# Two modulation vectors moved behind the recurrent stage, row vectors through DRAM, and norm operands made by ScalarE

## The chip, the cores and the metric

The kernel runs as one program on one core of one Trainium2 chip. The metric is the device time of one execution in microseconds (us). The engines named here are TensorE (PE in the profile), VectorE (DVE), ScalarE (ACT), GpSimd (POOL) and the queue of SyncE (SP), which only issues transfers from DRAM.

## The reference, cut to what matters

Two models of two layers each run one after the other on 256 tokens of 1024 channels, in fp32.

```python
# first model, layer 0; layer 1 has shared_kv + attention in place of rglru_mixer
mod = silu(c) @ mod_w[l] + mod_b[l]                      # (1, 6*1024)
sh_m, sc_m, g_m, sh_f, sc_f, g_f = split(mod, 6)
h = rmsnorm(x, norm_mix[l]) * (1 + sc_m) + sh_m
mix = rglru_mixer(h, ...)     # h@w_in, conv of 4, gates, a recurrence over tokens, @w_out
x = x + g_m * mix
h = rmsnorm(x, norm_ffn[l]) * (1 + sc_f) + sh_f
x = x + g_f * swiglu(h, ...)  # h@w_gate, h@w_up, @w_down
# second model, each layer: eight norms that have a gain and no shift
f = swiglu_2(rmsnorm_2(h, g[0]), ...);  h = h + 0.5 * rmsnorm_2(f, g[1])
mix = hybrid_mixer(rmsnorm_2(h, g[2]), ...);  h = h + rmsnorm_2(mix, g[3])
f = swiglu_2(rmsnorm_2(h, g[4]), ...);  h = h + 0.5 * rmsnorm_2(f, g[5])
gate = sigmoid(rmsnorm_2(h, g[6]) @ w_ple_gate[i])
h = h + rmsnorm_2((p[i] @ w_ple[i]) * gate, g[7])
```

Fourteen modulation vectors come out of `silu(c)`: six for each layer of the first model and two for `shared_kv`. The kernel numbers them v0 to v13 (`MODS`, line 173). v0 and v1 are scale and shift of the first norm, v2 is the gate `g_m` of layer 0, v3 and v4 are scale and shift of its feed-forward norm, v5 its gate `g_f`; v6 and v7 belong to `shared_kv`, v8 to v13 to layer 1.

## The kernel before, in words

**Weights.** All weights are one stream of 266 chunks of 128x2048 f32 (1 MB each), loaded in order by SP into four slots (`raw<-in_ws`). Of each half chunk ScalarE makes the high part (`whi<-raw`), and VectorE the low part (`wlo<-raw,whi`); five slots of each. A product in fp32 is three matmuls: high by high, high by low, low by high. The activations that a matmul reads are split in the same way into one buffer, `xhl`.

**Stages.** They follow each other as the weight stream has them: `lx` (w_in, with the conv of 4), `lg` (gates), `ly` (the other half of w_in, with the recurrence), `lo` (w_out), `b0pl` (an embedding product that only layer 0 of the second model needs), `gu0`, `dn0` (feed-forward of layer 0), `b1pl`, `kv`, `kk`, `aq`, `ao` (attention of layer 1), `gu1`, `dn1`; and then, for each layer l of the second model, `b{l}gu0`, `b{l}dn0`, `b{l}vd`, `za`, `zb`, `kn`, `vm`, `q`, `b{l}o`, `b{l}gu1`, `b{l}dn1`, `b{l}pg`. Stages like `lo`, `dn0`, `ao` end with a norm (a "boundary"): x is updated, normed, transposed on PE through a PSUM bank, multiplied by a gain (`gained`, 8 places in the second model, each for 2 token tiles and 2 halves) or by scale and shift (`modulate`), and split into `xhl`, which the first matmul of the next stage reads.

**The norm's operands.** `spread` (line 1065) does that last step. For a gain, VectorE multiplies 128x512 from the bank into a buffer `n`, ScalarE copies it to the high part (`xhl<-n`), VectorE subtracts for the low part. For scale and shift VectorE multiplies and adds; only four of these blocks, at the very start, are made by ScalarE in 128x128 pieces with scale and bias as pointers (`by_scalar`).

**Modulation vectors.** Each has a weight of 1024x1024 (`in_wm`), loaded 1 MB at a time into `raw` slots (for v0 and v1, in part, into tiles that the recurrent stage uses later, `part`). v0 to v4 are made by PE (`mod_pe`: groups of four products `bank<-raw,cs 32x512`), the others by VectorE. Columns (scale, shift) lie one channel a partition. Rows (the gates v2, v5, v10, v13, `MOD_ROW`) are wanted on all 128 partitions: `mod_row` accumulates on VectorE, and `row_sum` adds over partitions by fp32 matmuls with ones or halves, 128x512, two a vector. `JOBS` and `JOB_AT` (lines 174 and 176) set their order and the chunk at which each may begin.

**Order.** Nothing is issued as written. A `Recorder` collects all instructions, and `order` (line 481) places them by modelled costs (`cost_of`, `TABLE_LOAD`) and due times, each engine with its own list. Where PE's modelled wait is over 1 us and a PSUM bank is free, `keep_busy` (line 607) fills it with matmuls of ones on ones (`bank<-ones`), which compute nothing that is read; in the trace they stand at line 1253, two records for each instruction. Nearly all other instructions stand at line 687, the line of the recording helper, so the rows are told apart by operands.

**Paired units.** In `lx` a PSUM bank holds two units of 256 columns, of which `steps` evicts each as soon as its own sum is finished; the other unit's matmuls go to the same bank.

Of the kernel before, what the change touches and what calls it, by code (L numbers as in the profile page):

```python
# [108 lines left out]
def plan():  # L109
# [8 lines left out]
    for l in range(2):  # L118
        ph[f"b{l}pl"] = moving(2, lambda a, u, k, l=l: rows(a["w_ple_2"][l], k, span(u)), 1, 8)
        if l == 1:  # L120
            ph["kv"] = moving(KD, lambda a, u, k: rows(a["w_kv"], k, span(4 + u)))
            ph["kk"] = dense(4, KD, lambda a, u, k: rows(a["w_kv"], k, span(u)))
            ph["aq"] = dense(KD, KD, lambda a, u, k: rows(a["attn_w_q"][0], k, span(u)))
            ph["ao"] = moving(KD, lambda a, u, k: rows(a["attn_w_o"][0], k, span(u)), 1, 8)
        ph[f"gu{l}"] = gate_up("ffn_w_gate", "ffn_w_up", l)
        ph[f"dn{l}"] = moving(KF, lambda a, u, k, l=l: rows(a["ffn_w_down"][l], k, span(u)), 1, 8)
# [45 lines left out]
JOBS = [(0, 0), (1, 0), (0, 1), (1, 1), (2, 0), (2, 1), (3, 0), (3, 1), (4, 0), (4, 1)]  # L172
JOBS += [(v, 0) for v in (6, 7, 8, 9, 5, 10, 11, 12, 13)]
JOB_AT = [0, 0, 0, 0, 5, 5, 5, 5, 5, 5, 18, 22, 26, 30, 35, 41, 46, 51, 66]
# [7 lines left out]
def mod_stream(a):  # L182
    out = []
    for v, i in MOD_PART:
# [4 lines left out]
        elif v in MOD_ROW:  # L189
            w = w.reshape(4, 2, P, D)  # L190
        else:
            w = w.T.reshape(4, 2, P, D)
# [190 lines left out]
class Recorder:  # L383
# [97 lines left out]
    def order(self):  # L481
# [49 lines left out]
        while total:  # L531
            best = None
            for e, lst in pending.items():
                tmin, cand = None, []
                for o in lst[:48]:
# [5 lines left out]
                    if o.table and not o.table & table:  # L541
                        t += TABLE_LOAD
# [17 lines left out]
            t, e, o = best  # L560
            if o.table:
                table = table & o.table or set(o.table)
            total -= 1
            pending[e].remove(o)
            o.start, o.end = t, t + o.cost
# [165 lines left out]
class Program:  # L731
# [15 lines left out]
    def memory(self, ctx):  # L747
# [12 lines left out]
        self.pls = dram.tile([4, P, D], FT, name="pls")  # L760

# [117 lines left out]
    def start_job(self):  # L879
# [4 lines left out]
        return self.mod_row(v) if v in MOD_ROW else self.mod_col(v)  # L884
# [22 lines left out]
    def mod_row(self, v):  # L907
        nc = self.nc
        acc = self.row()
        bias = None  # L910
        for part in range(4):
            raw = self.mod_raw(v, 0, part, 0.0)
            if part == 3:
                bias = [self.mod_bias(v, h) for h in range(2)]
            for s in range(2):
                k = part * 2 + s
                w, col = raw[:, s * D:(s + 1) * D], self.cs[:, k:k + 1]
                if k == 0:
                    nc.vector.tensor_scalar(acc, w, col, None, op0=OP.mult)
                else:  # L920
                    nc.vector.scalar_tensor_tensor(acc, w, col, acc, op0=OP.mult, op1=OP.add)
            if part < 3:
                yield
        for h in range(2):
            self.row_sum(v, h, acc[:, h * 512:(h + 1) * 512], self.ones if MODS[v][2] == 2 else self.halves, acc,
                         bias[h])

    def mod_bias(self, v, h):
        b = self.wide()
        i = 9 + MOD_ROW.index(v)  # L930
        self.nc.sync.dma_start(b[:1], self.ins["rows"][i:i + 1, h * 512:(h + 1) * 512])
        return b

    def row_sum(self, v, h, acc, by, out, b):

        nc = self.nc
        nc.vector.tensor_add(acc[:1], acc[:1], b[:1])
        ps = self.bank()
        nc.tensor.matmul(ps, by, acc, start=True, stop=True)
        nc.scalar.activation(out[:, h * 512:(h + 1) * 512], ps, AF.Copy)  # L940
        self.mod_rows[v] = out

# [6 lines left out]
    def mod_pe(self, v, i):  # L949
# [4 lines left out]
        bias = self.mod_bias(v, i) if v in MOD_ROW else None  # L954
# [4 lines left out]
        self.mod_sums(v, i, ps, bias)  # L959

    def mod_sums(self, v, i, ps, bias=None):
# [16 lines left out]
    def mod_done(self, v, sums, o, n):  # L978
# [5 lines left out]
        if (kind == "kv" and j == 1) or (kind == "m" and j in (1, 4)):  # L984
            g = self.vec("kn", o, n) if kind == "kv" else self.vec("nm" if j == 1 else "nf", l * 8 + o, n)
            nc.vector.scalar_tensor_tensor(m, m, 1.0, g, op0=OP.add, op1=OP.mult)

# [21 lines left out]
    def steps(self, name, x, evict, at=lambda k, u: k, each=1):  # L1009
# [3 lines left out]
        seen, ps = {}, {}  # L1013
        for j, (u, k) in enumerate(p.order):
# [10 lines left out]
            if seen[u] == p.nk:  # L1025
                evict(u, ps[u][:, :T])
                yield u
# [27 lines left out]
    def turned(self, t, src, outs, k0=0):  # L1055

        self.spread(t, self.transposed(src), outs, k0)
# [7 lines left out]
    def spread(self, t, xt, outs, k0, by_scalar=False):  # L1065
        nc = self.nc
        n = xt.shape[1] // P
        for dst, g, sh in outs:
            u = xt[:, :n * P]
            bc = lambda c: c[:, k0:k0 + n, None].to_broadcast([P, n, P])  # L1070
            if by_scalar:
                v = self.wide(n * P)
                for j in range(n):
                    a = slice(j * P, (j + 1) * P)
                    nc.scalar.activation(v[:, a], u[:, a], AF.Identity, scale=g[:, k0 + j:k0 + j + 1],
                                         bias=sh[:, k0 + j:k0 + j + 1])
# [870 lines left out]
```

## Time and profile before

| | |
|---|---|
| time, median of 3 runs | 1696.34 us (1695.57 to 1697.22) |
| profiled execution | 1695.63 us, span 1693.8 us |
| granted TensorE clock, mean | 0.999 |
| busy share PE, DVE, ACT, POOL | 98%, 70%, 52%, 4% |
| matmuls of ones on ones | 248 records (124 instructions) |
| DMA | 353.02 MB, 208 GB/s mean |
| stage `lx` | 27.7 to 70.7 us of the span |
| stage `ly` | 89.7 to 130.7 |
| stage `lo` | 130.7 to 164.5 |
| stage `b0pl` | 164.5 to 173.8 |
| stage `gu0` | 173.8 to 305.8 |
| stage `ao` | 436.5 to 464.8 |

A busy PE is any matmul, those of ones included. Times of stages were read from PE's own order of instructions. The columns of the views are told at each group of rows below.

### The profile page before, as it was taken

To read this page: it belongs to the slowest core of one execution; us is meant where nothing else is said; L and a number is where in the kernel's file an instruction comes from. 1 tells how busy PE (TensorE), PEld (TensorE's weight loads), DVE (VectorE), ACT (ScalarE), POOL (GpSimd) and SP (SyncE) were. 2 spreads that over 40 slices of the span, in tenths; PEclk is the share of its full clock that TensorE was granted. 3 is DMA by queue.
4 is the path that set the end of the run, shared out by engine and by line. 5 is a ranking of instruction groups with operands and counts; after the bars stand their busy time and mean duration, and the time that the engine had idled before them with its cause. 6 is when DMAs were issued, how large, how long until landed. Compare 5 with 4: busy or idle time off the path is not lost.

```text
span 1693.8 us, 22563 instructions
## 1 busy us (share of the span) xinstructions
PE 1663.0 (98%) x8698; PEld 1383.3 (82%) x8698; DVE 1180.3 (70%) x1912; ACT 878.3 (52%) x1319; POOL 65.0 (4%) x97
## 2 busy tenths in 40 slices
PE   7999999999999999999999999999999999999997
PEld 4887888779878887888889788887888889888886
DVE  3879999888786656666478866548665477865646
ACT  3785444455644445455367544437544356554434
POOL 0000000010000000000000100001000000000001
PEclk9999999999999999999999999999999999999999
DMA  9577799986465554555442565445555542365451
GB/s 390 201 291 264 295 358 350 356 306 228 149 232 182 195 178 168 207 191 180 168 175 88 183 227 199 174 174 188 204 180 182 191 174 88 150 239 196 174 199 62
DMA packets 51019, 353.02 MB, mean 208 GB/s; under 512 B 5957, under 2 KB 6093, under 8 KB 9696
## 3 DMA queue, kind: packets, MB, share of 16 engines
q1 hardware_dynamic: 46960, 338.73, 54.2%
q0 software_dynamic: 3520, 11.60, 2.0%
q8 instruction: 68, 1.11, 0.3%
q10 hardware_dynamic: 432, 1.26, 0.2%
q14 instruction: 39, 0.32, 0.1%
HBM read 348.41 MB, written 3.16 MB: 208 GB/s over the span
## 4 chain that ended last, share of the span: by engine, by line
PE 64%; DVE 5%; issue 1%; ACT 1%; DMA 0%; POOL 0%; POOLq 0%; DVEq 0%; ACTq 0%
PE bank L687 64%; DVE wlo L687 2%; DVE n L687 1%; DVE x L687 1%; DVE xhl L687 0%; ACT n L687 0%; DMA raw<-in_wm_dram 0%; DVE macc L687 0%; ACT whi L687 0%; DVE part L687 0%; POOL sm L687 0%; DVE sm L687 0%; POOLq L1943 0%; DVEq L1943 0%; ACT xhl L687 0%
## 5 line engine op out<-in xcount | busy, mean ns | idle before, releaser
L687 DVE TENSOR_TENSOR wlo<-raw,whi 128x1024 fp32r<-128x1024 f32 (+1 forms) x577 | 651.6, 1139 | 372.3 <-ACT whi L687 370.5
L687 ACT ACTIVATE whi<-raw 128x1024 fp32r<-128x1024 f32 (+1 forms) x577 | 565.2, 992 | 539.4 <-PE bank L687 483.3
L687 PE MATMUL bank<-whi,xhl 128*128 128x512 f32 x2208 | 703.0, 394 | 1.7 <-DVE xhl L687 0.8
L687 PEld LDWEIGHTS bank<-whi,xhl 128*128 128x128 f32 x2208 | 413.1, 188 | 91.8 <-DVE xhl L687 4.5
L687 PE MATMUL bank<-whi,part 128*128 128x512 f32 x1464 | 460.4, 392 | 0.0
L687 PE MATMUL bank<-wlo,xhl 128*128 128x512 f32 x1104 | 431.7, 391 | 2.5 <-DVE wlo L687 2.2
L687 PEld LDWEIGHTS bank<-whi,part 128*128 128x128 f32 x1464 | 274.4, 188 | 58.6 <-ACT part L687 1.4
L687 PE MATMUL bank<-wlo,part 128*128 128x512 f32 x732 | 286.2, 392 | 1.2 <-DVE wlo L687 1.0
L687 PEld LDWEIGHTS bank<-wlo,xhl 128*128 128x128 f32 x1104 | 207.5, 188 | 47.2 <-DVE wlo L687 6.0
L687 PEld LDWEIGHTS bank<-wlo,part 128*128 128x128 f32 x732 | 137.6, 188 | 30.4 <-DVE wlo L687 2.5
L687 PE MATMUL bank<-xhl,whi 128*128 128x256 f32 x768 | 144.8, 287 | 0.0
L687 PEld LDWEIGHTS bank<-xhl,whi 128*128 128x128 f32 x768 | 120.4, 191 | 10.9 <-issue 6.4
L687 PE MATMUL bank<-xhl,wlo 128*128 128x256 f32 x384 | 108.9, 286 | 2.6 <-ACT part L687 2.6
L687 ACT ACTIVATE n<-bank 128x512 f32<-128x512 f32 (+2 forms) x116 | 60.4, 531 | 85.0 <-PE bank L687 81.8
L687 POOL TENSOR_TENSOR sm<-sm,mhalf 128x1 f32<-128x1 f32 (+1 forms) x52 | 41.8, 810 | 1339.3 <-DVE sm L687 1232.1
L687 PE MATMUL bank<-ident,n 128*128 128x128 f32 x512 | 81.8, 276 | 4.2 <-DVE n L687 4.2
L687 PEld LDWEIGHTS bank<-ident,n 128*128 128x128 f32 x512 | 63.2, 143 | 23.8 <-DVE n L687 7.0
L687 PEld LDWEIGHTS bank<-xhl,wlo 128*128 128x128 f32 x384 | 73.4, 191 | 4.0 <-ACT part L687 3.4
L687 ACT ACTIVATE part<-bank 128x512 fp32r<-128x512 f32 (+3 forms) x96 | 50.0, 528 | 39.5 <-PE bank L687 37.9
L687 DVE TENSOR_TENSOR part<-bank,part 128x512 fp32r<-128x512 f32 (+3 forms) x122 | 65.5, 551 | 3.4 <-PE bank L687 2.9
L687 DVE SCALAR_TENSOR_TENSOR n<-n,bank 128x512 f32<-128x512 f32 (+1 forms) x82 | 50.0, 612 | 12.8 <-ACT n L687 12.7
L687 DVE CUSTOM_DVE_ANT_0 raw<-raw,macc 128x1024 f32<-128x1024 f32 x48 | 57.1, 1221 | 0.1
(155 smaller groups left out, 1156.2 us busy)
## 6 DMA issues: line engine op xcount, KB each, us to landing
raw<-in_ws_dram SPq DMA_DIRECT2D x266, 1024.0 KB, 4.8
raw<-in_wm_dram SPq DMA_DIRECT2D x48, 1024.0 KB, 6.9
part<-in_wm_dram SPq DMA_DIRECT2D x8, 1024.0 KB, 12.9
macc<-in_rows_dram POOLq DMA_DIRECT2D x10, 512.0 KB, 4.3
pls<-n POOLq DMA_DIRECT2D x8, 256.0 KB, 4.4
macc<-pls POOLq DMA_DIRECT2D x4, 512.0 KB, 5.8
x<-in_x_dram ACTq DMA_DIRECT2D x2, 512.0 KB
n<-scr POOLq DMA_DIRECT2D x8, 128.0 KB, 7.0
```

What stands on the lines that cost most here:

```text
L687: getattr(getattr(rec.nc, name), method)(*[real(v) for v in args], **{k: real(v) for k, v in kw.items()})
```

## The change

1. The work of v3 and v4 leaves the job list. Their weights are loaded after the recurrent tiles come free: four parts into these tiles (`through`), four into `raw` slots, and their products, sums and the norm's operands are written behind `lo`. The stage `b0pl` moves from behind `lo` to behind `ao`, in the weight stream too.
2. All four row vectors are made as columns and spread: GpSimd writes the columns to a DRAM scratch `modr` (elements of 4 bytes) and reads it back as one row for 128 partitions. `mod_row`, `row_sum` and their bias loads go.
3. `steps` with two units in a bank evicts both when both are finished.
4. `spread` for a gain: ScalarE makes the high part from the bank in four 128x128 pieces with the gain as a pointer, VectorE the low part in four pieces. For scale and shift at a `turn_x` boundary ScalarE makes four pieces with two pointers in place of VectorE's multiply and add.
5. The scheduler charges the load of an activation table to the instruction that needs it, in place of delaying that instruction as a candidate.

```diff
-JOBS = [(0, 0), (1, 0), (0, 1), (1, 1), (2, 0), (2, 1), (3, 0), (3, 1), (4, 0), (4, 1)]
+JOBS = [(0, 0), (1, 0), (0, 1), (1, 1), (3, 0), (4, 0), (3, 1), (4, 1), (2, 0), (2, 1)]
...
-                    if o.table and not o.table & table:
-                        t += TABLE_LOAD
                     cand.append((t, o))
...
+            load = TABLE_LOAD if o.table and not o.table & table else 0.0
+            o.start, o.end = t, t + load + o.cost
...
@@ mod_done
+        if v in MOD_ROW:
+            if j == 5:
+                nc.vector.tensor_scalar(m, m, 0.5, None, op0=OP.mult)
...
+            dst = bass.AP(tensor=self.modr.tensor, offset=self.modr.offset + i * D + o * P, ap=[[1, P], [P, n]])
...
+            nc.add("gpsimd", lambda: self.nc0.gpsimd.dma_start(dst, m.real()), [row], [m], 0.6, 3.0)
+            if o + n == KD:
+                self.mod_rows[v] = self.row()
+                src = bass.AP(tensor=self.modr.tensor, offset=self.modr.offset + i * D, ap=[[0, P], [1, D]])
...
@@ steps
-            if seen[u] == p.nk:
-                evict(u, ps[u][:, :T])
-                yield u
+            if seen[u] < p.nk:
+                continue
+            done.append(u)
+            if each == 1 or all(seen.get(v, 0) == p.nk for v in range(u - u % each, u - u % each + each)):
+                for v in done:
+                    evict(v, ps[v][:, :T])
+                    yield v
+                done = []
@@ spread
+            if g is not None and sh is None:
+                for a, k in cols:
+                    nc.scalar.activation(hi[:, a], u[:, a], AF.Copy, scale=g[:, k])
+                    nc.vector.scalar_tensor_tensor(lo[:, a], u[:, a], g[:, k], hi[:, a].bitcast(FT), op0=OP.mult,
+                                                   op1=OP.subtract)
+                continue
...
@@ lru
-        then = self.modulate([(h, self.mod("m", 0, 4), self.mod("m", 0, 3))], 8.0)
+        through = [b.flat()[:, :CH * P] for b in (tt, ig, q, xc)]
...
+        load(4)
...
         self.natural("lo", Tall(yh), self.add_gated(gate, then), halves=2, tail=self.TAIL)
-        self.embed(0)
+        load(8)
+        out = [(h, *(self.mods[:, v * 8:(v + 1) * 8] for v in (3, 4)))]
+        for i in range(2):
+            for v in (3, 4):
+                ps = self.bank()
+                for part in range(2):
+                    self.mod_products(ps, raw[v, i, part], part)
+                self.mod_sums(v, i, ps)
...
```

What this does to the order is shown at three places. On PE, from the end of `lo` to the first matmuls of `gu0` (those that read `xhl`), before and after. `wlo_73` in `b0pl`'s rows is the buffer that holds its token operand; `cs` is `silu(c)`.

```order
L687 MATMUL bank_132<-whi_71,part_4_165 128x512
L687 MATMUL bank_136<-macc_128,sm_94 8x384
L1253 MATMUL bank_134<-ones 128x128 x10
L687 MATMUL bank_134<-whi_67,wlo_73 128x512
L687 MATMUL bank_134<-wlo_72,wlo_73 128x512
L687 MATMUL bank_131<-whi_67,wlo_73 128x512
```

```order
L687 MATMUL bank_136<-wlo_74,wlo_73 128x512
L687 MATMUL bank_136<-whi_68,wlo_73 128x512
L687 MATMUL bank_130<-ident,n_115 128x128 x4
L687 MATMUL bank_133<-ident,n_116 128x128 x4
L1253 MATMUL bank_135<-ones 128x128 x12
L687 MATMUL bank_135<-whi_69,xhl_77 128x512
```

```order
L685 MATMUL bank_136<-whi_71,part_4_166 128x512
L685 MATMUL bank_132<-ident,n_118 128x128 x4
L685 MATMUL bank_129<-part_3_165,cs 32x512 x4
L685 MATMUL bank_129<-part_0_162,cs 32x512 x4
L685 MATMUL bank_130<-raw_66,cs 32x512 x3
L685 MATMUL bank_134<-ident,n_113 128x128 x4
L685 MATMUL bank_130<-raw_66,cs 32x512
L685 MATMUL bank_130<-raw_64,cs 32x512
L685 MATMUL bank_135<-ident,n_111 128x128 x4
L685 MATMUL bank_130<-raw_64,cs 32x512 x3
L685 MATMUL bank_133<-ident,n_114 128x128 x4
L685 MATMUL bank_131<-raw_63,cs 32x512
```

The first fence is the end of `lo` and the start of `b0pl`, the second the end of `b0pl` and the start of `gu0`, with 10 and 12 matmuls of ones; the third is the same place in the changed kernel, where products of v3 and v4 and the norm's transposes stand behind `lo`, and neither `b0pl` nor a matmul of ones.

On the queue of SP, the transfers that reach from `ly` to `gu0` (`in_wm` is a modulation weight, `in_ws` the stream; `part_0` to `part_3` are the recurrent tiles).

```order
L687 DMA raw_63<-in_ws_dram 128x2048
L687 DMA raw_65<-in_wm_dram 128x2048
L687 DMA raw_64<-in_wm_dram 128x2048
L687 DMA raw_66<-in_wm_dram 128x2048
L687 DMA raw_63<-in_ws_dram 128x2048
L687 DMA raw_65<-in_ws_dram 128x2048
```

```order
L685 DMA raw_65<-in_ws_dram 128x2048
L685 DMA part_1_163<-in_wm_dram 128x2048
L685 DMA part_2_164<-in_wm_dram 128x2048
L685 DMA part_3_165<-in_wm_dram 128x2048
L685 DMA part_0_162<-in_wm_dram 128x2048
L685 DMA raw_66<-in_wm_dram 128x2048
L685 DMA raw_64<-in_wm_dram 128x2048
L685 DMA raw_63<-in_wm_dram 128x2048
L685 DMA raw_66<-in_wm_dram 128x2048
L685 DMA raw_64<-in_ws_dram 128x2048
```

Before, modulation weights lie between chunks of the stream; in the changed kernel eight of them stand in one run, behind the last chunk of `lo` and ahead of the first of `gu0` (`raw_64<-in_ws`, last row).

On PE, from `b0pg` to `b1gu0`, a boundary with a gain, before and after (`x` is the updated residual, `xhl_77` the next stage's operand).

```order
L687 MATMUL bank_136<-whi_69,part_0_7267 128x512
L1253 MATMUL bank_131<-ones 128x128 x4
L687 MATMUL bank_131<-ident,x 128x128 x4
L687 MATMUL bank_129<-ident,x 128x128 x4
L1253 MATMUL bank_133<-ones 128x128 x8
L687 MATMUL bank_133<-whi_70,xhl_77 128x512
```

```order
L685 MATMUL bank_133<-whi_69,part_0_7308 128x512
L1232 MATMUL bank_130<-ones 128x128 x4
L685 MATMUL bank_130<-ident,x 128x128 x4
L685 MATMUL bank_129<-ident,x 128x128 x4
L685 MATMUL bank_134<-whi_70,xhl_77 128x512
L685 MATMUL bank_134<-wlo_76,xhl_77 128x512
```

The eight matmuls of ones between the transposes and the first matmul of the next stage are gone. Over the whole program the matmuls of ones fall from 124 instructions to 51, the fp32 row sums from 8 to none, and PE's transposes of `n` rise from 512 to 520; ScalarE gets 1392 instructions in place of 1216, VectorE 1987 in place of 1914, GpSimd nine more transfers.

## Rows read from the trace of the kernel before

**Rows 1.** The page: span, and PE's busy time, share and instructions.
```profile
span 1693.8 us, 22563 instructions
PE 1663.0 (98%) x8698; PEld 1383.3 (82%) x8698; DVE 1180.3 (70%) x1912; ACT 878.3 (52%) x1319; POOL 65.0 (4%) x97
```

**Rows 2.** Windows: stretch, length; busy us (instructions) per engine; granted clock; DMA share; GB/s.
```profile
7.00:15.00 8.00, 3.87 (x16) 0.40 (x16) 2.77 (x19) 2.45 (x8) 0.56 (x1) 1.00 1.02 426
...
89.70:130.70 41.00, 40.77 (x322) 32.25 (x320) 31.14 (x68) 34.22 (x70) 0.04 (x1) 1.00 0.76 277
130.70:164.50 33.80, 33.80 (x175) 28.05 (x172) 31.58 (x61) 17.47 (x29) 1.58 (x3) 1.00 0.70 264
164.50:173.80 9.30, 9.30 (x60) 8.13 (x58) 8.19 (x17) 7.42 (x12) 2.77 (x5) 1.00 0.74 274
173.80:190.00 16.20, 15.90 (x84) 12.87 (x84) 15.74 (x26) 5.36 (x8) 2.15 (x1) 1.00 0.59 209
...
844.00:866.00 22.00, 21.29 (x110) 17.11 (x109) 20.22 (x37) 16.83 (x31) 2.10 (x4) 1.00 0.46 168
...
1176.10:1188.30 12.20, 12.20 (x57) 9.81 (x58) 10.79 (x28) 6.34 (x11) 3.13 (x4) 1.00 0.39 138
...
1686.00:1694.00 8.00, 0.00 (x0) 0.00 (x0) 2.87 (x5) 1.05 (x3) 0.86 (x1) 0.71 0.28 108
```

**Rows 3.** Timeline, 53.0 to 54.3 (`lx`): start, duration, engine, instruction, idle before, releaser.
```profile
53.41 0.56 ACT L687 ACTIVATE part<-bank,vecs 128x256 f32<-128x256 f32 x1 [1.51 <-PE bank L687]
...
54.03 0.39 PE L687 MATMUL bank<-xhl,wlo 128*128 128x256 f32 x1 [0.66 <-ACT part L687]
```

**Rows 4.** Timeline of PE, 160.5 to 164.9: between `lo` and `b0pl`.
```profile
162.29 2.50 PE L1253 MATMUL bank<-ones 128*128 128x128 f32 x20
164.54 0.47 PE L687 MATMUL bank<-whi,wlo 128*128 128x512 f32 x1
```

**Rows 5.** Groups of PE: records, busy us, mean ns of one, idle before.
```profile
L1253 PE MATMUL bank<-ones 128*128 128x128 f32 x248 | 30.9, 275 | 0.0
...
L687 PE MATMUL bank<-raw,cs 128*32 128x512 f32 x96 | 13.4, 602 | 0.2 <-DMA raw<-in_wm_dram 0.2
...
L687 PE MATMUL bank<-macc,halves 128*128 128x512 f32 x8 | 3.9, 605 | 0.4 <-DVE macc L687 0.4
```

**Rows 6.** Timeline of DVE, 148 to 151: the last scan of the recurrence.
```profile
148.93 0.70 DVE L687 TENSOR_TENSOR_SCAN n<-part,part 128x256 f32<-128x256 f32 x1
```

**Rows 7.** DMA issues: engine, count, KB each, median us from issue to landing.
```profile
raw<-in_wm_dram SPq DMA_DIRECT2D x48, 1024.0 KB, 6.9
...
macc<-in_rows_dram POOLq DMA_DIRECT2D x10, 512.0 KB, 4.3
```

**Rows 8.** Timeline of ACT, 24.4 to 26.9: the four blocks made by ScalarE.
```profile
24.46 1.51 ACT L687 ACTIVATE n<-bank,mods 128x128 f32<-128x128 f32 x4 [0.92 <-DVE mods L687]
25.85 1.16 ACT L687 ACTIVATE xhl<-n 128x512 fp32r<-128x512 f32 x2
```

**Rows 9.** Groups of ACT: the copy to the high part.
```profile
L687 ACT ACTIVATE xhl<-n 128x512 fp32r<-128x512 f32 x40 | 24.4, 629 | 17.3 <-DVE n L687 17.3
```

**Rows 10.** Groups of DVE: the norm's multiply and subtract, and the nearest small piece.
```profile
L687 DVE TENSOR_TENSOR xhl<-n,xhl 128x512 fp32r<-128x512 f32 x40 | 26.7, 688 | 1.0 <-ACT xhl L687 0.9
L687 DVE TENSOR_TENSOR n<-bank,vecs 128x512 f32<-128x512 f32 x40 | 26.1, 686 | 2.2 <-PE bank L687 2.1
...
L687 DVE CUSTOM_DVE_ANT_0 n<-bank,masks 128x128 f32<-128x128 f32 x32 | 9.0, 286 | 5.1 <-PE bank L687 5.1
```

**Rows 11.** Timeline, 1173.8 to 1177.5: from `b0pg` to `b1gu0`.
```profile
1173.97 1.28 DVE L687 TENSOR_TENSOR n<-bank,vecs 128x512 f32<-128x512 f32 x2
1174.00 1.95 PE L1253 MATMUL bank<-ones 128*128 128x128 f32 x16
...
1175.41 1.14 ACT L687 ACTIVATE xhl<-n 128x512 fp32r<-128x512 f32 x2
...
1176.08 0.50 PE L687 MATMUL bank<-whi,xhl 128*128 128x512 f32 x1
```

More of the change, by code (lines that the diff above doesn't have):

```diff
@@ L124, in plan @@
             ph["ao"] = moving(KD, lambda a, u, k: rows(a["attn_w_o"][0], k, span(u)), 1, 8)
+            ph["b0pl"] = moving(2, lambda a, u, k: rows(a["w_ple_2"][0], k, span(u)), 1, 8)
         ph[f"gu{l}"] = gate_up("ffn_w_gate", "ffn_w_up", l)
@@ L560, in order @@
             t, e, o = best
+            total -= 1
+            pending[e].remove(o)
+            load = TABLE_LOAD if o.table and not o.table & table else 0.0
+            o.start, o.end = t, t + load + o.cost
             if o.table:
                 table = table & o.table or set(o.table)
-            total -= 1
-            pending[e].remove(o)
-            o.start, o.end = t, t + o.cost
             if e == "tensor":
@@ L905, in mod_col @@
         self.mod_done(v, m, 0, KD)
[L907 to L941, printed above, removed]
     def mod_products(self, ps, raw, part):
@@ L1012, in steps @@
         p = PLAN[name]
-        seen, ps = {}, {}
+        seen, ps, done = {}, {}, []
         for j, (u, k) in enumerate(p.order):
@@ L1210, in modulate, with normed @@
     def modulate(self, outs, d=3.4):
-        def then(t, ss):
-            r = self.rstd(ss, 1.0 / D)[0]
-            srcs = []
-            for h in range(2):
-                v = self.wide()
-                self.nc.vector.tensor_scalar(v, self.xn(t, h), r, None, op0=OP.mult)
-                srcs.append(v)
-            self.turn_x(t, srcs, outs, d)
-        return then
+        return lambda t, ss: self.turn_x(t, self.normed(t, ss), outs, d)
+    def normed(self, t, ss):
+        r = self.rstd(ss, 1.0 / D)[0]
+        srcs = []
+        for h in range(2):
+            v = self.wide()
+            self.nc.vector.tensor_scalar(v, self.xn(t, h), r, None, op0=OP.mult)
+            srcs.append(v)
+        return srcs
     def gained(self, outs, d=3.6):
@@ L1300, in block1 @@
         ready(0)
-        self.n_job = 4
+        self.n_job = 8
         self.prefetch(1)
@@ L1404, in lru, with load, then @@
         h = self.xhl()
-        then = self.modulate([(h, self.mod("m", 0, 4), self.mod("m", 0, 3))], 8.0)
-        self.natural("lo", Tall(yh), self.add_gated(gate, then), halves=2, tail=self.TAIL)
-        self.embed(0)
+        through = [b.flat()[:, :CH * P] for b in (tt, ig, q, xc)]
+        parts = [(v, i, part) for i in range(2) for v in (3, 4) for part in range(2)]
+        raw = {}
+        def load(n):
+            for x in parts[len(raw):n]:
+                raw[x] = self.mod_raw(*x, 0.0, through[len(raw)] if len(raw) < 4 else None)
+        load(4)
+        srcs = {}
+        def then(t, ss):
+            srcs[t] = self.normed(t, ss)
+        self.natural("lo", Tall(yh), self.add_gated(gate, then), halves=2, tail=self.TAIL)
+        load(8)
[5 more added lines that the diff above has]
+                    self.mod_products(ps, raw[v, i, part], part)
+                self.mod_sums(v, i, ps)
+            if i == 0:
+                self.turned(0, srcs[0][0], out, 0, True)
+        for t, i in ((0, 1), (1, 0), (1, 1)):
+            self.turned(t, srcs[t][i], out, 4 * i, True)
         return h
```

62 lines of the change are left out of this document (28 added, 34 removed).

## The prediction, written before the changed kernel was run

> **What bounds the kernel now.** I read the page first [rows 1]: PE is busy 1663.0 of 1693.8 us, so the end is set by what stands in PE's queue, and there are two ways to gain: instructions taken out of that queue, and waits taken out of it. Busy is not useful: the groups of PE show 248 records of matmuls of ones on ones, 30.9 us, and fp32 row sums at 605 ns a record [rows 5]. Then the windows of each stage [rows 2]. What the reader is to see there is how far a stage lies above the same work undisturbed: the first unit of `b1gu0` takes 12.2 us, that of `gu0` 16.2 us with the same number of weights. VectorE is busy 31.6 of 33.8 us in `lo` and 20.2 of 22.0 at a later boundary, ScalarE 17.5 and 16.8 there, so VectorE is the engine that has nothing to spare at a boundary and ScalarE has a quarter. The timelines give single prices.
>
> The sum is made against the profiled execution: 1695.63 us, its span of 1693.8 and 1.8 around it. The median of the runs shown is 0.7 above that.
>
> **Prices.** One instruction of ones is two records; 20 records took from 162.29 to 164.54, so 0.225 us an instruction [rows 4]. The group of 8 records of row sums is busy 3.9 us, four instructions, so 0.98 each [rows 5]. A group of four products of v0 to v4 is 8 records: 13.4 us for 96 records is 1.1 us a group [rows 5]. A block of a norm on ScalarE in four pieces took 1.51 us [rows 8], the copy it replaces 0.63 [rows 9], so ScalarE pays 0.88 more. VectorE's multiply is 0.69 and its subtract 0.69 [rows 10]. Its new four pieces with a pointer are not in the trace; the nearest small piece is 0.286 [rows 10], four are 1.14; the other end is the multiply plus the subtract, 1.37. I take 1.3, a gain of 0.1, and count it as nothing; so VectorE is hardly helped at a gain, though its chain is shorter.
>
> **From `lx` to the start of `gu0` (part 1, 2 and 3).** Out of PE's queue before 173.8 go: `b0pl`, 9.3 us with its 12 instructions of ones [rows 2]; the 10 instructions of ones ahead of it, 2.25; of 13 in `lo` 10, 2.2; two row sums of v2, 1.9. The paired eviction takes out four waits like the one at 54.03, where PE idles 0.66 us because the bank's other half is being read by the eviction at 53.41 [rows 3]: 2.6. Products of v3 and v4 leave `ly` and come back behind `lo`, nothing on balance; eight transposes are added, 0.9. If PE had no other wait, `gu0` would start 17.4 us earlier, at about 156.4.
>
> It will have one. The four tiles in which half of the moved weights land are free only when the recurrence is done; its last scan ends at 149.6 now [rows 6]. SP issues in order, so the four loads into `raw` slots and the first chunk of `gu0` stand behind these. `ly` is shorter by eight groups of products, 8.8 us if PE were all that bounds it, and the scan also moves by the 2.6 of `lx`; VectorE, 31.1 of 41.0 us busy in `ly` [rows 2], leaves room for that. Of these 11.4 I take 10.1, so the scan ends near 139.5. One load of 1.05 MB at the highest rate shown, 426 GB/s [rows 2], is 2.5 us; seven of the eight behind the scan are 17.3, and 4.2 us for the landing's tail, the products, sums and first blocks of the norm (an estimate: 6.9 us from issue to landing [rows 7], of which 2.5 are the transfer itself). `gu0` then starts at 161.0, 12.8 earlier. The bounds are 17.4 (no wait) and 2.7 (the scan stays at 149.6, start at 171.1).
>
> **Behind that.** (a) `gu0`, 5 less: its first unit lies 4.0 us over the undisturbed one [rows 2], with PE waiting in pieces for a norm that is not finished; in the changed order the norm's halves are made one after the other behind the weights, the first one ahead of the first matmul, and I take 3.0 of the 4.0. Two row sums of v10, 1.9, go from the stage. (b) `dn0`: two row sums of v5, 1.7 after the wait ahead of them. (c) `ao` to `gu1`: `b0pl` comes in with 24 matmuls of 512 columns, 5.4 us, and nine instructions of ones, 2.0; against that go 18 instructions of ones, 4.0, two row sums of v13, 1.9, and waits for the norm in `gu1`'s first unit, which `b0pl` now covers: I take 0 on balance, bounds 2 less and 3 more. (d) `kv`, 8 instructions of ones, 1.8: 1.3. (e) Ahead of `b0gu0`, six instructions become fewer: 0.8. (f) From `b0pg` to `b1gu0`: 2.08 us lie between the transposes and the first matmul, filled with ones, while VectorE multiplies (1.28 for two) and ScalarE copies [rows 11]. With the gain on ScalarE the first piece ends about 0.46 us after the bank is ready, so 1.5 less. (g) The six other places with a gain: the chain loses one of two steps of 0.63 to 0.69, but VectorE and other work stand ahead; 0.4 each, 2.4 (bounds 0 and 1.0 each). These are 12.7 us.
>
> What is late next where a wait goes: at (f) and (g) the low part, VectorE's four pieces, which the second matmul group reads; at `gu0` the modulation loads themselves.
>
> Costs taken as nothing. The row through DRAM: two transfers a vector on GpSimd's queue, of which the trace shows only the broadcast read of a like row, 4.3 us [rows 7]. The write in 4-byte pieces is not shown. It is asked for at least one stage ahead of use (v2 is computed near chunk 5, used at the end of `lo`), and that stage is the cover. GpSimd waits in order at the write for the column and at the read for the write; behind them in its queue stand the small powers of the next norm, for which the whole boundary waits. Bounds: 0, and the whole of a chain of 10 us at one boundary if a vector is late. I take 0, since each row is due over 50 us after its sums. The table-load charge only moves ScalarE's order: between 1.3 less and 1.3 more, taken as 0.
>
> The Trainium skill's page "DMA: Bandwidth & Descriptors", section "Specifications", wants 512 bytes or more for line rate and says that smaller transfers go by read-modify-write. It speaks against the scratch write; no row before shows such a transfer's time, and at 4 KB a vector the sum is the same by either.
>
> **Sum.** 12.8 + 12.7 = 25.5 less: 1670.1 for the profiled execution, 1670.8 for the median.
>
> **Rivals.** *The loads decide (R1).* For: all eight loads are in one run behind tiles that come free last, and the first chunk of `gu0` is behind them. Against: PE's shorter `ly` should pull the scan forward. Then `gu0` starts at 171.1, the front gives 2.7, and the time is 1695.63 − 15.4 + 0.7 = 1680.9.
>
> *The ones were only covers (R2).* Where ones stood, PE waits for the same data without them; then (d), (e), (f), (g) and the 3.0 of (a) give nothing: 9.0 less gain, 1679.8. For: the scheduler puts ones only where its model sees a wait. Against: in `lo` and ahead of `b0pl` the next matmul follows at once [rows 4]. With R1 together, 1689.9.
>
> *ScalarE takes the boundary (R3, the slower side).* Each of the 32 blocks with a gain costs it 0.88 us more, 3.5 at a boundary, and those with scale and shift 1.5. If at the boundary its whi splits, which PE waits for, are pushed by all of that, eight places lose 28.2 us and (f) and (g) give no 3.9: 25.5 − 3.9 − 28.2 is 6.6 slower, 1702.9. It decides from the point where ScalarE's idle time at a boundary is under 3.5 us; the row at 844 has 22.0 − 16.8 = 5.2 [rows 2], with VectorE's multiply as the later one. So unlikely.
>
> The Trainium skill's page "ScalarE: Activation LUTs", section "Rules for kernel authors", speaks for it: multiply and add are VectorE's, and an ACTIVATE has about 0.3 us of fixed cost and 0.83 ns an element. By that, four pieces of 128 are an estimated 1.6 us; the trace has 1.51 with two pointers, so it nearly agrees, and ScalarE would pay 3 us more over all 32 blocks, within its idle time.
>
> *The clock falls (R4).* With 73 fewer instructions of ones PE idles more. The granted clock was 0.71 in the last 8 us, after the last matmul, yet 1.00 from 7 to 15 us, where PE was busy only 3.87 of 8.0 [rows 2]. If it fell to the lower level (1.2 GHz) and cost 2 us at each of 14 boundaries, 28.0 would be lost and the time 1699. Against it: that row has 4.1 us of idle PE at the full clock, and the gaps in question are 1 to 4 us.
>
> **How the numbers follow.** Forecast 0.57, R1 0.14, R2 0.13, both 0.06, R3 0.05, R4 0.03, and 0.02 for a row vector that is late. Some 0.2% (3.4 us) is what a measurement of this kernel tells from no change. Forecast, R1, R2 and both lie over that: 0.90. The edges of "both" (6.4 less) and of the slow ones give 0.04 to no change and leave 0.06 slower. The likeliest case alone reaches from 34 less (17.4 in front, and 16.7 behind with (a) at 5.9, (c) and (g) at their good ends and the rest as taken) to 16 less (half of the sum's parts at their bad ends), 1662 to 1680. The range goes from 1660 to 1689: R1 and R2 alone are in it, both together mostly not, R3 and R4 not.
>
> **What would show it.** `gu0` starting near 161 with the last scan near 139.5; eight transfers of `in_wm` 2.5 us apart ahead of it; no idle of about 0.7 us at `lx`'s evictions; `gu0`'s first unit near 13; the first matmul of `b1gu0` some 0.6 us behind its transposes; the clock 1.00 in every window. The forecast is wrong if the scan stays near 149.6, if `whi` splits are what PE waits for at the boundaries with a gain, or if waits of PE grow by as much as the ones shrink.

## The result

The changed kernel takes 1709.13 us (median of 4; 1708.91 to 1712.49) against 1696.35: 1.008 times as long, interval 1.0062 to 1.0097. The forecast was 1670.8, faster: the sign was wrong, and the time by 38 us.

The page of the changed kernel, to be read beside [rows 1]:

```profile
span 1707.1 us, 22470 instructions
PE 1651.8 (97%) x8544; PEld 1372.9 (80%) x8544; DVE 1151.2 (67%) x1985; ACT 911.3 (53%) x1495; POOL 68.9 (4%) x106
```

PE is busy 11.2 us less, in a span 13.3 longer: work went out of PE's queue as forecast, and 24.5 us of waits came in. Lengths of the stages, taken from PE's own order in each trace, tell where (us; `b0pl` is counted with the stages that it stands between):

| stages | before | changed | forecast |
|---|---|---|---|
| lx, lg | 61.9 | 61.5 | shorter by 2.6 |
| ly | 41.0 | 50.1 | 32.2 (8.8 less) |
| lo and b0pl; lo alone after | 43.1 | 46.3 | 41.7 (the rest of 12.8) |
| gu0 | 132.0 | 125.1 | 127 |
| dn0 | 65.6 | 77.7 | 63.9 |
| b1pl, kv | 20.3 | 24.2 | 19 |
| ao, gu1; ao, b0pl, gu1 after | 162.1 | 158.4 | 162.1 |
| b0pg | 28.5 | 25.9 | 27.0 |

`ly` and `dn0` lose 21 us; all else together gains 8. The chain of waits of the changed kernel, in `ly` (start, us, what):

```profile
88.63 17.99 DMA modr<-mods
...
107.74 8.67 DMA macc<-in_rows_dram
...
116.43 0.02 ACT macc L685
...
117.39 1.04 ACT whi L685
```

and the timeline of GpSimd there (idle before, releaser in brackets):

```profile
82.28 0.81 POOL L951 DMA_DIRECT2D modr<-mods  x1 [65.80 <-DVE mods L685]
88.63 0.76 POOL L951 DMA_DIRECT2D modr<-mods  x1 [5.54 <-DVE mods L685]
107.19 0.56 POOL L956 DMA_DIRECT2D macc<-modr  x1 [17.80 <-DMA modr<-mods]
107.74 0.55 POOL L685 DMA_DIRECT2D macc<-in_rows_dram  x1
```

The second half of v2, 2 KB in 512 pieces of 4 bytes, takes 18 us to land. GpSimd waits for it before it issues the read of the row; behind that in its queue stands the load of the row `c`, the input of the model that ScalarE turns into `silu(c)` on all partitions for VectorE's modulation vectors. In the kernel before that load was issued at 16.99, 90 us earlier, and in e1 below, without the scratch, at 16.38:

```profile
16.99 0.56 POOL L687 DMA_DIRECT2D macc<-in_rows_dram  x1
```

So part 2 did not only put a wait ahead of this load, it also moved the load from the start into `ly`. ScalarE and PE, in the timeline of the changed kernel:

```profile
116.43 1.06 ACT L685 ACTIVATE macc<-macc 128x1024 f32<-128x1024 f32 x1 [16.45 <-DMA macc<-in_rows_dram]
117.39 1.04 ACT L685 ACTIVATE whi<-raw 128x1024 fp32r<-128x1024 f32 x1
...
118.49 0.80 PE L685 MATMUL bank<-xhl,whi 128*128 128x256 f32 x2 [9.09 <-ACT whi L685]
```

ScalarE stands 16.45 us at the silu of that row with the `whi` splits queued behind it, and PE waits 9.09 for them. In `dn0` the chain of waits has no scratch transfer in it; there it runs over the weight chunks themselves, two of which land in over 14 us where the median is 4.8:

```profile
324.71 14.40 DMA raw<-in_ws_dram
...
344.98 14.93 DMA raw<-in_ws_dram
```

The scratch writes of v5 and v10 were issued at 322.7 and 345.4, just beside these. Windows of the changed kernel (columns as in [rows 2]):

```profile
109.00:118.00 9.00, 0.40 (x4) 0.20 (x2) 0.48 (x1) 1.57 (x2) 0.00 (x0) 0.66 0.67 279
118.00:122.00 4.00, 2.86 (x11) 2.57 (x12) 3.62 (x6) 4.00 (x11) 0.54 (x1) 0.50 0.06 15
330.00:340.00 10.00, 5.65 (x25) 4.33 (x24) 2.98 (x5) 0.79 (x1) 1.63 (x3) 1.00 0.76 191
340.00:350.00 10.00, 9.61 (x34) 7.30 (x35) 7.18 (x9) 4.22 (x6) 0.91 (x1) 0.83 1.02 420
350.00:360.00 10.00, 8.98 (x40) 7.11 (x38) 4.41 (x5) 1.01 (x2) 1.73 (x4) 1.00 0.72 104
```

In 330 to 340 and 350 to 360 the DMA engines are 0.76 and 0.72 busy and move 191 and 104 GB/s, where 420 went at a share of 1.02 in 340 to 350: while the small pieces are on their way the engines carry little. The clock column shows a second cost: after PE's 9 us of waiting the granted clock is 0.50, the lower level of 1.2 GHz, for 118 to 122.

Two things that the forecast asked for can be read at once. In `lx` the wait is still there, [rows 3] line for line:

```profile
53.23 0.56 ACT L685 ACTIVATE part<-bank,vecs 128x256 f32<-128x256 f32 x1 [1.51 <-PE bank L685]
...
53.84 0.39 PE L685 MATMUL bank<-xhl,wlo 128*128 128x256 f32 x1 [0.66 <-ACT part L685]
```

And from `b0pg` to `b1gu0`, against [rows 11], the first matmul follows 0.51 us after the second block's transposes began, with no ones:

```profile
1189.34 0.42 PEld L685 LDWEIGHTS bank<-ident,x 128*128 128x128 f32 x4 [0.24 <-DVE x L685]
1189.44 0.61 ACT L685 ACTIVATE xhl<-bank,vecs 128x128 fp32r<-128x128 f32 x2
...
1189.85 0.50 PE L685 MATMUL bank<-whi,xhl 128*128 128x512 f32 x1
```

### The profile page after: what moved, and what is told of

Read it like the earlier page. It is cut to its first block, busy times and chain, and to the rows that moved or that the text cites. A ratio compares the mean times of both kernels' runs of the same rounds, so it can differ in the third digit from the quotient of the medians.

```text
span 1707.1 us, 22470 instructions
## 1 busy us (share of the span) xinstructions
PE 1651.8 (97%) x8544; PEld 1372.9 (80%) x8544; DVE 1151.2 (67%) x1985; ACT 911.3 (53%) x1495; POOL 68.9 (4%) x106
## 4 chain that ended last, share of the span: by engine, by line
PE 87%; DMA 5%; DVE 3%; ACT 2%; issue 1%; POOL 0%; ACTq 0%; POOLq 0%; DVEq 0%
PE bank L685 86%; DMA raw<-in_ws_dram 3%; DVE wlo L685 2%; DMA modr<-mods 1%; ACT whi L685 1%; ACT n L685 1%; DMA x<-in_x_dram 1%; ACT part L685 1%; DMA macc<-in_rows_dram 1%; DVE n L685 0%; DVE raw L685 0%; PE bank L1232 0%; DMA raw<-in_wm_dram 0%; DVE part L685 0%; DVE xhl L685 0%
## 5 line engine op out<-in xcount | busy, mean ns | idle before, releaser
L685 PEld LDWEIGHTS bank<-wlo,part 128*128 128x128 f32 x732 | 138.6, 189 | 30.9 <-DVE wlo L685 1.7
L685 PE MATMUL bank<-xhl,whi 128*128 128x256 f32 x768 | 149.1, 293 | 13.1 <-ACT whi L685 12.6
L685 PEld LDWEIGHTS bank<-xhl,whi 128*128 128x128 f32 x768 | 124.3, 197 | 20.6 <-ACT whi L685 14.1
L685 DVE CUSTOM_DVE_ANT_0 raw<-raw,macc 128x1024 f32<-128x1024 f32 x72 | 85.4, 1219 | 10.7 <-DMA raw<-in_wm_dram 10.7
```

Of the source, the lines that this page charges most:

```text
L685: getattr(getattr(rec.nc, name), method)(*[real(v) for v in args], **{k: real(v) for k, v in kw.items()})
```

## The experiments

Theory S: the scratch writes in 4-byte pieces hold up the weight stream and what stands behind them on GpSimd's queue. Rival M: the moved modulation loads overload the DMA engines. Times are medians. The kernel before, timed beside each, took 1695.8 to 1697.0; ratios are to it, with their 95% interval. Parts are numbered as in the change.

**e1, part 2 undone.** The changed kernel with `mod_row`, `row_sum` and bias loads as before:

```diff
-        return self.mod_col(v)
+        return self.mod_row(v) if v in MOD_ROW else self.mod_col(v)
```

> The changed kernel with part 2 undone: row vectors are again made by mod_row / row_sum (8 fp32 row sums on PE), nothing goes through the DRAM scratch. Theory S (the 4-byte writes to the scratch hold up the weight loads; they cost ly +9, lo +3, dn0 +12, b1pl and kv +4): ly falls from 50.1 to about 30, dn0 from 77.7 to about 63 to 66, time 1709 - 26 + 7 (row sums back) = 1687 to 1693. Theory M (the moved modulation weights and their new order overload the DMA engines in ly, lo and dn0): the stages stay as long, time 1705 or more.

1678.1 us, 0.990 (0.9884 to 0.9914). `ly` is 29.1, `dn0` 66.8. M falls: the moved loads and their order are all there. Against the changed kernel 31.0 us are gained, though eight row sums came back. The time is 9 us under the range that I expected: `ly` had lost 21.0 us to the scratch, and I had counted 9.

**e2, pieces of 512 bytes.**

```diff
-            dst = bass.AP(..., ap=[[1, P], [P, n]])
+            dst = bass.AP(..., ap=[[P, n], [1, P]])
...
+            nc.tensor.transpose(pm, m, self.ident)
+            nc.scalar.activation(flat, pm, AF.Copy)
...
```

> The changed kernel, but each vector's columns are first transposed on PE (128x8 to 8x128), copied by ScalarE and written to the scratch as rows of 512 bytes: 8 pieces in place of 1024. Everything else as changed. S: a write lands in under 4 us (12 to 18 with the 4-byte pieces), ly about 30, dn0 about 62, time 1678 to 1686. M: 1703 or more. If the round trip through DRAM itself is at fault (write, wait, read on one queue), and not the size of the pieces, ly stays above 45.

1683.2 us, 0.993 (0.9911 to 0.9944). The issues of the writes of 4 KB, in the changed kernel and in e2 (the last figure is the median from issue to landing):

```profile
modr<-mods POOLq DMA_DIRECT2D x3, 4.0 KB, 12.5
...
modr<-n POOLq DMA_DIRECT2D x3, 4.0 KB, 5.9
```

`dn0` is 66.8 as in e1. `ly` is 31.3 and `lo` 50.6, 2.2 and 4.3 longer than in e1: the chain GpSimd, row c, ScalarE is still there, only shorter. Part of the length of `lo` is the clock, 0.76 in its first 11 us where e1 has 1.00:

```profile
119.00:130.00 11.00, 8.43 (x37) 6.88 (x38) 10.74 (x24) 10.09 (x24) 0.00 (x0) 0.76 0.28 96
```

S holds; the landing was slower and `dn0` longer than I wrote.

**e3, part 2 alone on the kernel before.**

> The kernel before with part 2 alone (columns, 4-byte writes to the scratch, broadcast read). S: dn0 becomes 10 to 14 us longer and the stage in which v2 is written 6 to 12 longer, row sums give back 7: 1704 to 1715. M: the row sums are gone and nothing else changes, 1688 to 1692.

1719.5 us, 1.014 (1.0128 to 1.0158): 23.7 slower, more than expected, with `ly` 60.0 (41.0 before) and `dn0` 74.2 (65.6). Part 2 alone makes the kernel slower; the other parts aren't needed for it.

**e4, the row c loaded by SP.** This divides the loss in `ly`.

```diff
-        self.crow = self.fixed_row(9)
+        g, r = self.row(), self.ins["rows"]
+        self.nc.sync.dma_start(g, bass.AP(..., ap=[[0, P], [1, D]]))
+        self.crow = g
```

> The changed kernel; only the load of the row c (macc<-in_rows, whose silu ScalarE computes in ly) goes from GpSimd's queue, where it stands behind the scratch write and read, to SP's. If the wait of 9.2 us in ly is GpSimd's order (write, read, row c, then ScalarE waits with the whi splits behind it): ly falls by 8 to 10, dn0 stays at 77.7, time 1698 to 1702. If it is the DMA engines themselves being held up by the 4-byte pieces: ly stays within 3 us, time 1706 to 1710.

1701.6 us, 1.0036 (1.0023 to 1.0049): 7.6 less than the changed kernel. `ly` is 41.2, down by 8.9 as expected of GpSimd's order, but still 12 over e1; `dn0` stays at 77.1. On SP's queue the load itself is late beside the scratch write, and ScalarE still waits 4.6 us for it:

```profile
macc<-in_rows_dram SPq DMA_DIRECT2D x1, 512.0 KB, 20.9
```

So both mechanisms are in `ly`, GpSimd's order and late transfers, and only the second in `dn0`.

**e11 and e12, writes that nobody reads.** These are e1 with four added writes of 4 KB on GpSimd's queue, of the columns v6 to v9 as soon as each is done; the order on PE, VectorE, ScalarE and SP is that of e1. e12 writes the same bytes as 128 pieces of 32 bytes.

```diff
+        if v in (6, 7, 8, 9):
...
+            dst = bass.AP(..., ap=[[1, P], [P, n]])      # e12: ap=[[n, P], [1, n]]
+            nc.add("gpsimd", lambda: self.nc0.gpsimd.dma_start(dst, m.real()), [row], [m], 0.6, 3.0).soon = True
...
```

(`soon` has the scheduler place a write right behind its columns.)

> e1 (row vectors by PE, 1678.1 us, no scratch) with four 4-byte scratch writes added on GpSimd's queue, as soon as the columns v6, v7, v8 and v9 are done, that nobody reads or waits for; the order of all instructions on PE, DVE, ACT and SP is the same. Theory S, contention alone (while 1024 pieces of 4 bytes are on their way, weight chunks land late): each write in gu0 or dn0, where the weight stream keeps the DMA engines 0.9 busy, costs 3 to 6 us, together 1688 to 1702, chunk loads of 10 us and more beside them. Rival (the loss comes only from those who wait for the write or stand behind it in GpSimd's queue): 1677 to 1680.

1697.8 us, 19.7 more than e1; ratio 1.001 (1.0 to 1.002). Of this 19.3 are in `dn0`, 86.1 for 66.8, where the writes fell (291 to 317). GpSimd's timeline shows how closely they follow:

```profile
310.68 0.90 POOL L995 DMA_DIRECT2D modr<-mods  x1 [18.43 <-DVE mods L690]
315.17 0.88 POOL L995 DMA_DIRECT2D modr<-mods  x1 [3.59 <-DVE mods L690]
316.49 0.89 POOL L995 DMA_DIRECT2D modr<-mods  x1 [0.44 <-DVE mods L690]
```

The chain of waits in that stage runs over two weight loads of 1 MB, whose medians are 7.0 and 4.8 us (start, us, what):

```profile
292.28 14.81 DMA raw<-in_wm_dram
...
318.60 24.58 DMA raw<-in_ws_dram
```

Another chunk is late too: ScalarE waits 17.00 us for it, and PE 11.08 for ScalarE's split of it:

```profile
334.13 2.00 ACT L690 ACTIVATE whi<-raw 128x1024 fp32r<-128x1024 f32 x2 [17.00 <-DMA raw<-in_ws_dram]
...
335.24 1.22 PE L690 MATMUL bank<-whi,part 128*128 128x512 f32 x2 [11.08 <-ACT whi L690]
```

GpSimd itself waits 13.8 us, in two places, for these writes to land before it issues loads (`n<-scr`); none of those loads is in this stage's chain. The window with the last three writes has the DMA engines busy all the time at half the rate (380 GB/s at a share of 0.98 from 345 to the stage's end), and the clock at 0.83, which is 1.00 in all of e1's `dn0`. So a part of the 19.7 us comes by way of the clock:

```profile
309.20:335.20 26.00, 14.95 (x59) 11.92 (x59) 11.14 (x13) 5.09 (x6) 6.43 (x10) 0.83 1.00 182
```

The issues of the four writes in e11:

```profile
modr<-mods POOLq DMA_DIRECT2D x4, 4.0 KB, 16.3
```

> As e11 (e1 with four scratch writes that nobody waits for, the same order on all engines), the same 4 KB in each write, but laid out so that a partition's eight columns go as one piece of 32 bytes: 128 pieces in place of 1024. If the price goes by pieces: an eighth of e11's 19.7 us, so 2 to 3, 1679 to 1682, and the writes land in under 5 us. If it goes by the write (any write below some size, or GpSimd's queue beside SP's): 1692 to 1698, as e11.

1678.2 us, 0.989 (0.9875 to 0.9908), where e1 took 1678.1. Such an interval alone would hardly tell 2.5 us, an eighth of e11's loss, from nothing; the stage does, with `dn0` 66.84 in both. The issues in e12:

```profile
modr<-mods POOLq DMA_DIRECT2D x4, 4.0 KB, 5.1
```

Queue and bytes are the same, and the moments nearly (289.9 to 309.3 for 291.3 to 316.5); only the pieces differ. So the delay of other transfers is shown by itself: on average 4.9 us a write in this stage. The price went to nothing, not to an eighth, so it isn't proportional to the count of pieces; where between 4 and 32 bytes (or 1024 and 128 pieces) it begins was not measured.

**e5, the eviction of a pair forced.** The edit is made on e1:

```diff
-            nc.scalar.activation(o, ps[:, :T], AF.Identity, scale=cw(3), bias=self.vec("cb", u))
+            nc.scalar.activation(o, ps[:, :T], AF.Identity, scale=cw(3), bias=self.vec("cb", u), after=self.last_mm)
```

(`last_mm` is the last matmul of the pair.)

> The changed kernel with part 2 undone (1678.1 us), and in lx the eviction of both units of a bank made to depend on the pair's last matmul. Theory: part 3 as written orders nothing, since the scheduler still places the first unit's eviction ahead of the second unit's last matmul, which then waits 0.81 us at the same bank; forced, four such waits go: 1674.5 to 1675.5. Rival: PE waits as long at the next pair, since that needs the evicted operand's slots: 1677.5 to 1679.

1675.2 us, 0.9875 (0.986 to 0.989), 2.9 less than e1. `lx` is 39.3 for 42.9, and no wait of 0.8 is left in it. In e1, with part 3 as written, the waits were there; with the dependence they are gone. So the written order was not the order that the scheduler issued, and a dependence was needed to get it.

**e6, no matmul of ones.** `keep_busy` is never called.

```diff
-                if self.idle and free[e] and t - free[e] > 1.0:
+                if False:
```

> The kernel before without any matmul of ones. As predicted (a part of the ones stands where the next matmul could follow at once): the 33 such instructions in lx, lo, ahead of b0pl and in gu0 give back 3 to 7 us, 1689 to 1693. Only covers: 1695 to 1697. The clock falls where PE now idles (as it did in the changed kernel after its 9 us wait in ly): 1698 or more, with a granted clock under 1 behind the waits of over 2 us.

1696.8 us, ratio 1.000 (0.9991 to 1.0009). My expectation of 3 to 7 us was wrong: without the 124 instructions, 30.9 us of busy PE, the kernel takes the same time. But this null is a sum of gains and losses, which the stages tell apart.

The gain is in `lo`, 2.2 us shorter. Ahead of `b0pl` PE starts 1.04 us behind the last matmul of `lo`, where it was 2.99 with ten instructions of ones between ([rows 4] has their end; its `macc,sm` matmul starts at 161.55):

```profile
162.88 0.81 PE L687 MATMUL bank<-macc,sm 33*8 33x384 f32 x2
...
163.92 0.50 PE L687 MATMUL bank<-whi,wlo 128*128 128x512 f32 x1 [0.23 <-ACT wlo L687]
```

There the ones held a matmul back. At the boundaries they only covered a wait: from `b0pg` to `b1gu0` the next stage's first matmul starts at the same distance as in [rows 11], within 0.03 us, and now shows the wait:

```profile
1176.13 0.50 PE L687 MATMUL bank<-whi,xhl 128*128 128x512 f32 x1 [1.90 <-ACT xhl L687]
```

The loss is `ly` (1.3 longer, where a modulation load comes later), `b1gu0` (1.7) and `gu1` (0.9). In part it is the clock, which falls where the ones are missing (first the kernel before with 1.00, then e6 with 0.89):

```profile
460.00:490.00 30.00, 28.55 (x146) 22.05 (x145) 27.83 (x38) 15.42 (x21) 2.70 (x2) 1.00 0.66 238
```

```profile
460.00:490.00 30.00, 24.72 (x94) 17.98 (x93) 28.13 (x37) 14.43 (x21) 3.25 (x3) 0.89 0.64 247
```

In the kernel before the granted clock is 1.00 until its last matmul. In e6 it is at its lower level in five stretches, together 17 us, each behind waits of PE of about 2 to 3 us where ones stood; here are two of them, and then the second one's window in the kernel before:

```profile
174.00:177.40 3.40, 3.11 (x8) 2.39 (x8) 3.40 (x8) 0.53 (x2) 1.07 (x1) 0.50 0.76 281
...
1177.50:1180.90 3.40, 3.40 (x10) 2.65 (x9) 2.96 (x5) 1.29 (x4) 1.23 (x1) 0.51 0.00 0
```

```profile
1177.50:1180.90 3.40, 3.40 (x17) 2.74 (x16) 2.96 (x5) 1.35 (x4) 1.17 (x1) 1.00 0.00 0
```

In the last pair PE does 10 matmuls for 17 in the same time. So ones gave something back where they kept the clock up and took something where they stood ahead of ready work; in the whole these cancel. How much each came to was not separated.

**e7, part 4 alone.**

> The kernel before with part 4 alone (norm operands by ScalarE from the bank). As predicted by (f), (g) and half of (a): 4 to 6 us faster, 1690 to 1692. Rival R3 (ScalarE takes the boundary): slower, 1697 or more, with PE waiting for whi at the boundaries.

1686.7 us, 0.9941 (0.9925 to 0.9958), 10.3 faster (interval 7.1 to 12.7; its profiled execution 8.3), about twice what was expected. `gu0` is 3.3 shorter, `gu1` 3.8, `b0pg` 2.5; no other stage gains more than 1.2. R3 falls. The pieces cost less than my nearest rows said (groups of the changed kernel, busy us and mean ns):

```profile
L685 ACT ACTIVATE xhl<-bank,vecs 128x128 fp32r<-128x128 f32 x96 | 27.4, 374 | 2.4 <-PE bank L685 1.2 <-DVE xhl L685 0.6
```

27.4 / 96 is 0.29 us for one piece, 1.14 for four, against 1.51 with two pointers [rows 8].

**e8, part 1 alone, and e9, parts 1 and 5.**

> The kernel before with part 1 alone (v3 and v4 behind lo, b0pl behind ao, new job order). As predicted: gu0 starts 8 to 11 us earlier, b0pl takes 7 back behind ao less what it covers, 1685 to 1689. Rival R1: gu0 starts at 171 or later, 1692 or more.

1703.6 us, 1.0042 (1.0027 to 1.0057): slower, and outside what I expected. PE's timeline shows why, at the end of `ly`:

```profile
118.20 19.81 PE L1255 MATMUL bank<-ones 128*128 128x128 f32 x176
137.77 0.48 PE L688 MATMUL bank<-whi,part 128*128 128x512 f32 x1
```

> The kernel before with parts 1 and 5 (moved vectors, and the table load charged to its instruction). e8 (part 1 alone) lost in ly, where the order has 88 instructions of ones in one run; with part 5 the order has none there. If that run is modelled wait only and the data are ready: ly falls from 48.4 to about 29, lo starts near 119, time 1686 to 1690 (e1 without the norm's and 10 us that e7 measured). If the 88 stood for a true wait (the loads of rival R1): PE waits there instead, time 1700 to 1704.

1689.1 us, 0.9959 (0.9944 to 0.9974). The 88 instructions of ones are not in its order, `ly` is 29.1 for 48.4, and the same matmul starts at 119.03, without a wait:

```profile
119.03 0.39 PE L687 MATMUL bank<-whi,part 128*128 128x512 f32 x1
```

So they covered a wait that existed only in the scheduler's model. Part 5, a few lines on a table load of 1.3 us, is worth 14.5 us with part 1; alone on the kernel before it was not run.

**e10, both halves of the mechanism mended.** The changed kernel with e2, e4 and e5.

> The changed kernel with rows of 512 bytes for the scratch (e2), the row c loaded by SP (e4) and the forced pair in lx (e5). S, with both halves of its mechanism repaired: ly 29 to 30, lo 46 to 48, time 1671 to 1675, at or under e5's 1675.2, since the row sums are gone (dn0 and gu1 1 to 2 us shorter). If the round trip through DRAM still costs a wait: 1677 to 1681.

1673.5 us, 0.9868 (0.9854 to 0.9883): 35.6 less than the changed kernel and the fastest here, but not to be told from e5 by its interval. `gu1` is 126.5 and `dn0` 66.3 (127.4 and 66.8 in e5) without row sums; `lo` is 49.0 (46.3), a little more than expected, with what is left of the round trip in it.

## Why the prediction was wrong

**The step that failed** is the one costed at nothing: "I take 0, since each row is due over 50 us after its sums". The time from sums to use was right, and it answers the wrong question. It hides the wait of the reader. It does not hide what the transfer does to others while it runs. e1 against the changed kernel puts 31.0 us there, e3 against before 23.7, and e11 gives 19.7 with no reader at all. The prediction bounded this by "a chain of 10 us at one boundary", which looked only at those waiting. It had the size of the transfers before it and put it aside, the sum being the same "by either" since the bytes are few; the count of pieces was not asked for. The Trainium skill's page "DMA: Bandwidth & Descriptors", section "Rules for kernel authors", says that a last dimension that isn't contiguous becomes one descriptor an element. The traces here can't show that: their DMA packets rise by 128 over e1 in e11 and in e12 alike. What the runs do show is that the price hangs on the pieces: 19.7 us with 4 bytes (e11), nothing with 32 (e12).

**The queue.** I named GpSimd's order and put the norm's powers behind the write. What stood behind was the load of the row c, on whose silu ScalarE waits with the weight splits behind it. Taking it off that queue gave 7.6 us (e4).

**The paired eviction** (2.6) gave nothing. The first unit's eviction still stood ahead of the second unit's last matmul. "That the change doesn't do what it says" was not among my rivals. Forced, it gave 2.9 (e5).

**The ones** (in `lo`, ahead of `b0pl`, and in (a), (c), (d), (e)) were both things, each at its place. Ahead of `b0pl`, 2.25 of the sum, e6 gives 1.95: there they held a matmul back. The 2.2 in `lo` came to 0.3, and at the boundaries R2 was right, they were covers. I read "the next matmul follows at once" [rows 4] as a sign that it had been ready. It is none: the order puts it behind the ones whether ready or not, and [rows 11] shows the same at a place where they were covers. In e8 88 of them cost 19 us, where the wait was only in the model. Whether ones cost anything depends on the wait being real, and a row of ones doesn't say. That PE loses clock without them, as in e6, was not in the sum.

**The front.** Without the scratch (e1), `gu0` starts at 165.5 (161.0 forecast), 8.3 earlier for 12.8, and the loads into the freed tiles begin at 135.5 (scan forecast 139.5). From 123.8 on PE runs `lo`, products and transposes nearly without a wait, so R1 falls, and my chain of loads was not the bound either: PE was, 9 us behind my floor of 156.4. 2.6 of the 9 are the evictions' waits and 1.9 v2's row sums, which e1 has back. At the start of `lo` PE waits for the last of the recurrence; the row of e1 has it busy for 8.9 of 11 us:

```profile
119.00:130.00 11.00, 8.91 (x38) 6.44 (x37) 10.99 (x21) 8.67 (x16) 0.00 (x0) 1.00 0.46 158
```

And the products of v3 and v4, "nothing on balance", take 10.3 us behind `lo` where they took 8.9 in `ly`. Those are 3.5 more; the last us I did not trace.

**The boundaries.** (a) was about right: in e7 `gu0` is 3.3 shorter for 3.0. (f) was too small, 2.5 for 1.5. `gu1`, whose wait for the norm (c) gave to `b0pl` to cover, is 3.8 shorter in e7, where `b0pl` doesn't stand ahead of it; that was not in e7's expectation and is most of what it missed. (g) was too large: the stages around its six places got about 1.5 shorter together, for 2.4. DVE's multiply and ScalarE's copy went out of the chain, and ScalarE's four pieces cost 0.51 more than the copy, not 0.88. In the changed kernel `ao`, `b0pl` and `gu1` are together 3.7 shorter, outside (c)'s bound of 2.

**Part 5** was taken as 0, between 1.3 less and 1.3 more; with part 1 it is worth 14.5. It was priced as an engine's work and was a change of the order.

**The clock** (R4) fell, but not for fewer ones: e1 has 40 instructions of them, fewer than the changed kernel's 51, and a mean clock of 0.999 for 0.990. The changed kernel's falls lie behind its long waits in `ly` and `dn0`; how much of the 31.0 us is theirs was not separated. Gaps of 1 to 4 us, which I held safe, were not safe in e6, where the clock fell behind waits of 2 to 3 us.

**The sum.** By its parts it was near without the scratch: 25.5 less the 5.5 put down to the row sums of v5, v10 and v13 is 20.0 (v2's 1.9 stand only in the 17.4, not in the 12.8), and e1 measured 17.7. That is luck in part: the front gave 4.5 less, the stages from `ao` to `gu1` and `b0pg` gave more. The range's better end was also added wrongly: its own terms behind the front are 19.2, not 16.7, so 36.6 less and not 34.

## What to carry to other kernels

Ask of every added transfer what it does to the transfers beside it, not only whether its reader can wait; a 4 KB write in 4-byte pieces cost this kernel about 5 us in a stage whose weight stream fills the DMA engines, and the same bytes in pieces of 32 cost it nothing. List what stands behind each new wait in an in-order queue down to the engine that feeds the bottleneck. Where a scheduler orders the work, look into its order for the edit itself: here a reordering in the source did nothing, and a change to the cost rule gave more time than any other part that was measured. A null result of a whole kernel can be two effects that cancel: look at its stages before you call a cause worth nothing.

## What was not expected of the hardware

v13's scratch write in `gu1`, issued at 533.3, cost PE nothing: `gu1` was 126.9 us, 128.6 in e1 with two row sums. The windows of the changed kernel, the whole of `gu1`, the write in it, and `dn0`:

```profile
488.60:615.60 127.00, 125.96 (x578) 103.85 (x578) 84.59 (x97) 66.21 (x83) 4.84 (x9) 1.00 0.69 236
...
533.00:546.00 13.00, 13.00 (x63) 10.79 (x62) 7.36 (x9) 6.50 (x7) 1.45 (x2) 1.00 0.84 102
...
310.50:388.20 77.70, 69.46 (x278) 54.03 (x276) 53.92 (x82) 27.33 (x35) 8.79 (x15) 0.93 0.92 318
```

During the write the engines moved 102 GB/s here too, yet PE was busy for all of the 13 us. The likely reading is that with a mean share of 0.69 the stream has room to be late and with 0.92 in `dn0` it has none; this is one write in one stage, and no run moved it. What in the engines is held up for so long by pieces of 4 bytes, the runs do not show.
